# Causal mask added on VectorE with the maximum; loads in a new order; 37 warm-up matmuls instead of 27

## The chip, the cores and the metric

The kernel runs on one core of a Trainium2 chip. The metric is the device time of one execution in microseconds (us), the median of several runs. The engines of the core work in parallel, each through its own list of instructions in order: TensorE (PE) multiplies matrices, VectorE (DVE) and ScalarE (ACT) do element-wise work and reductions, GpSimd (POOL) small helpers, and SyncE (SP) issues most transfers from the main memory (HBM). PE writes its results to PSUM; everything else lies in SBUF.

## The reference

A decoder trunk of two layers for 256 positions of width 1024, in float32:

```python
for i in range(DEPTH):
    if i % N_MIXERS == 0:                    # layer 0: gated chunks
        u, v, q_mem = split(x @ a_w_in)
        mix = gmlp_mixer(u, v, ...)          # gelu(u) * (W_s LayerNorm(gelu(v)) + b) in chunks of 128
    else:                                    # layer 1: causal attention, 12 heads of 64
        q, k, v, q_mem = split(x @ b_w_in)
        mix = moba_attention(q, k, v)        # 256 positions are one key block: plain causal softmax
    mem_out = memory_cross_attention(q_mem, mem, w_mem_kv[i])   # 4 heads, 256 memory tokens
    sub = concat([mix, mem_out]) @ w_mix_out[i]
    x = layer_norm(ALPHA * x + sub, ...)
    x = layer_norm(ALPHA * x + swiglu(x, w_ffn_in[i], w_ffn_out[i]), ...)
```

In the causal attention a score counts only where the key's position is not behind the query's: `s_own = where(k_pos <= q_pos, s_own, -inf)`, then a softmax over the keys.

## The kernel before

Matrix products are made exact enough by splitting each float32 operand into a high and a low part: ACT rounds a raw tile to the high part (L370, `CAST`), DVE subtracts to get the low part (L371, `TENSOR_TENSOR`), and PE multiplies high by high, high by low and low by high. So each weight byte passes HBM, then ACT, then DVE, then PE. A class `Stream` loads weights in units of 1 MB (`raw_...`) into four raw buffers and splits them by halves into ten buffers (`spl_...`). A raw buffer is free again when DVE has done the low parts of both its halves.

The program, in the order of PE's work:

- 27 warm-up matmuls on a tile of zeros (L405).
- `va`: the v part of the first projection, 8 steps of 12 matmuls. Its weights and the transposed input come together in `raw_v0` to `raw_v3`, which fill the four raw buffers; `x0T` is the split input.
- `hqm` from unit `qm0` (queries of the memory attention; their split tiles are `qqm`), `pu` from `u0`, `u1`, `u2`, then `hkm` from `km0` (memory keys), `sv` (the spatial gating), the memory attention, and the output projection `opa` with units `o0_...`.
- the FFN of layer 0 (tiles ending in `f`), then layer 1: `bv`, `hqm` again, six rounds of two heads (`qk`, `s`, `pt`, `pv`), the output projection `opc`, and the FFN (tiles ending in `g`).

Besides the weights there are small inputs: the memory (`mraw` from `memT`, four loads of 256 KB), the spatial weights `wsT` (768 KB), scale and shift of the inner norm (`gv`), and six pieces of bias (`bs`). `memT` is needed by `hkm`, `wsT`, `gv` and the biases by `sv` and the steps around it.

In a round of the causal attention, `scores` computes for each of two heads a tile `s` in PSUM: the first 128 queries against keys 0 to 127 in columns 0 to 127, the other 128 queries against all 256 keys in columns 128 to 383. Columns 0 to 127 and 256 to 383 hold a triangle to be masked. The mask is `maskb`, 0 or -1e30 in bf16, added by one more matmul with the identity matrix `identb` that closes the accumulation. `Softmax` then takes the negated maximum of each part on DVE (`mb`), the exponential on ACT with that maximum as bias and with the sum of the row read out (`pb`, `zb`), and `normalise` scales by the reciprocal on DVE. The transposes `pt` of a round come a round later.

PE's order is the program's. The order of DVE, ACT and SP is set by three tables of numbers, `VECTOR_ORDER`, `SCALAR_ORDER` and `SYNC_ORDER`: each lists the instructions of its engine, by their number in the program, in the order in which they are to stand; `keep_order` enforces it. An instruction that waits therefore holds all that stand behind it.

Of the kernel before, what the change touches and what calls it, by code (L numbers as in the profile page):

```python
# [13 lines left out]
F32 = mybir.dt.float32  # L14
F32R = mybir.dt.float32r
BF16 = mybir.dt.bfloat16
AF = mybir.ActivationFunctionType
ALU = mybir.AluOpType
# [3 lines left out]
P = 128  # L22
# [10 lines left out]
WARM = 27  # L33
# [5 lines left out]
NEG = -1e30  # L39

# [147 lines left out]
class Stream:  # L188
# [169 lines left out]
def build(nc, tc, ins, out):  # L358
    ET = mybir.EngineType
    with (  # L360
# [12 lines left out]
        def acc_tile(name):  # L373
            return ps.tile([P, 512], F32, tag="acc", name=name)

        def mm_tile(name):
            return ps.tile([P, 512], F32, tag="mm", name=name)

        def work_tile(name):
            return actp.tile([P, 512], F32, tag="work", name=name, bufs=9)  # L380

        def sm(name, n=1):
            return small.tile([P, n], F32, tag=f"sm{n}", name=name, bufs=2 if n > 2 else 8)
# [4 lines left out]
        def flat(s):  # L388
            return s.rearrange("p a b -> p (a b)") if len(s.shape) == 3 else s
# [3 lines left out]
        def mm(o, lhsT, rhs, start, stop, on=False):  # L393
            nc.tensor.matmul(o, lhsT, rhs, start=start, stop=stop, skip_group_check=on)  # L394
# [8 lines left out]
        wt = mm_tile("warmup")  # L403
        for i in range(WARM):
            nc.tensor.matmul(wt[:, :P], warm, warm, start=True, stop=True)  # L405
        ident = const.tile([P, P], F32, name="ident")
        make_identity(nc, ident)
        identb = const.tile([P, P], BF16, name="identb")
        nc.gpsimd.tensor_copy(identb, ident)
        maskb = const.tile([P, 1, P], BF16, name="maskb")  # L410
        nc.gpsimd.memset(maskb, 0.0)
        nc.gpsimd.affine_select(
            out=maskb, in_=maskb, compare_op=ALU.is_ge, fill=NEG, base=0,
            pattern=[[0, 1], [-1, P]], channel_multiplier=1)
# [46 lines left out]
        class LayerNorm:  # L461
            def __init__(self, tt, xres, acc, nm):
                self.tt, self.r, self.acc, self.nm = tt, xres[tt], acc, nm
                self.stats = sm(f"st{nm}{tt}", 18)
                self.n = 0
# [45 lines left out]
        class Softmax:  # L511
            def __init__(self, s, parts, nm):
                self.p, self.parts = work_tile(f"p{nm}"), parts
                self.z = sm(f"z{nm}", 2)
                m = sm(f"m{nm}", 2)
                if len({hi - lo for lo, hi in parts}) == 1:
                    nc.vector.tensor_reduce(m, s.rearrange("p (n k) -> p n k", n=len(parts)), AX.X, ALU.max, negate=True)
                else:
                    for i, (lo, hi) in enumerate(parts):
                        nc.vector.tensor_reduce(m[:, i:i + 1], s[:, lo:hi], AX.X, ALU.max, negate=True)  # L520
                for i, (lo, hi) in enumerate(parts):
                    nc.scalar.activation(self.p[:, lo:hi], s[:, lo:hi], AF.Exp, bias=m[:, i:i + 1], accum_out=self.z[:, i:i + 1])
# [346 lines left out]
        for i in range(4):  # L869
# [11 lines left out]
            out=wsT, in_=wsT, compare_op=ALU.is_ge, fill=0.0, base=0,  # L881
            pattern=[[0, 12], [1, P]], channel_multiplier=-1)
# [20 lines left out]
        for j in range(4):  # L903
            t = actp.tile([P, 2, 512], F32R, tag="hm", name=f"memT{j}", bufs=4)
# [12 lines left out]
        for jj in range(3):  # L917
# [7 lines left out]
            bias = bsB[jj].rearrange("p (j o) t -> p j o t", o=1).to_broadcast([P, 2, 2, P])  # L925
# [78 lines left out]
        def scores(hp):  # L1004
            st, kl = qks[hp]
            ss = []
            for par in range(2):
                s = acc_tile(f"s{hp}{par}")
                q, k = st[:, 0, par, :], st[:, 1, par, :]
                mm(s[:, 0:128], q[:, 0:128], k[:, 0:128], True, False)  # L1010
                mm(s[:, 0:128], q[:, 0:128], kl[:, par, 0:128], False, False)
                mm(s[:, 128:384], q[:, 128:256], k, False, False)
                mm(s[:, 128:384], q[:, 128:256], kl[:, par], False, False)
                mm(s.rearrange("p (b t) -> p b t", t=256)[:, :, 0:128], identb, maskb.to_broadcast([P, 2, P]), False, True)
                ss.append(s)
            return [Softmax(s, [(0, 128), (128, 384)], f"b{hp}{j}") for j, s in enumerate(ss)]
# [149 lines left out]
```

## Time and profile before

| | us |
|---|---|
| median of 3 runs | 576.11 (575.17 to 577.29) |
| the profiled execution, its own time | 576.19 |
| its span from first to last instruction | 574.5 |
| PE busy | 554.3 |
| DVE busy | 502.7 |
| ACT busy | 379.0 |
| POOL busy | 48.7 |

The times in rows of the profile are microseconds from the start of the span. A row of the timeline has the start, the duration, the engine, the line of the code, the operation, output and inputs, and in brackets how long the engine had been idle before and what released it. Rows that follow each other with the same form are merged (x46), and the duration is then that of all. `PEld` is PE's loading of weights, which runs beside its matmuls; `SPq` is SP issuing transfers. A row of windows has, for each engine, busy us and the number of instructions, and then the granted clock of PE (1.00 is full), the share of the DMA engines' time and the rate in GB/s.

### The profile page before, as it was taken

The page shows a single profiled execution, that of the slowest core. Times are in us where ns is not written, and L with a number is a line of the kernel's source. Part 1 is how long each engine was busy: PE and PEld are TensorE (multiplying, and loading weights), DVE is VectorE, ACT ScalarE, POOL GpSimd, SP SyncE. Part 2 cuts the span into 40 slices and gives each one's busy share as a digit, 9 for nine tenths or more (in the row PEclk, how much of TensorE's full clock was granted, in tenths as well). Part 3 has the DMA queues.
Part 4 walks back from the last instruction along what each step waited for, and adds up shares of the span by engine and source line. Part 5 has one row for each costly group of instructions (what it writes and reads, how often), then busy time and mean ns, then how long its engine had stood idle before and what let it go on. Part 6 is the DMA issues. An engine that isn't in the chain of part 4 may idle for free. (4 is left out here: it accounts for less than half of the span.)

```text
span 574.5 us, 8129 instructions
## 1 busy us (share of the span) xinstructions
PE 554.3 (96%) x3037; PEld 479.1 (83%) x3037; DVE 502.7 (88%) x665; ACT 379.0 (66%) x576; POOL 48.7 (8%) x62
## 2 busy tenths in 40 slices
PE   8799999999999999999999999999998999999994
PEld 7799978978888888888899999778787888888884
DVE  5588759999999999997988888469999999898986
ACT  6585565876777768684456887564858677685830
POOL 1100002010202010100000000010112020101001
PEclk9979999999999999999999999999999999999999
DMA  8998833739796959587378243055397959595702
GB/s 302 352 400 321 314 132 96 203 102 269 208 293 189 303 203 271 217 269 254 130 260 326 74 148 114 35 127 178 97 272 201 333 166 301 189 266 218 216 1 74
DMA packets 23496, 120.99 MB, mean 211 GB/s; under 512 B 2592, under 2 KB 4896, under 8 KB 13344
## 3 DMA queue, kind: packets, MB, share of 16 engines
q1 hardware_dynamic: 17264, 99.03, 44.8%
q0 software_dynamic: 5760, 20.97, 20.6%
q10 hardware_dynamic: 432, 0.46, 0.3%
q8 instruction: 24, 0.39, 0.3%
q14 instruction: 16, 0.13, 0.1%
HBM read 119.41 MB, written 1.05 MB: 210 GB/s over the span
## 5 line engine op out<-in xcount | busy, mean ns | idle before, releaser
L370 ACT CAST spl_s_M<-raw_s_T 128x1024 fp32r<-128x1024 f32 x80 | 82.1, 1051 | 33.8 <-DVE raw_s_T L250 25.2
L371 DVE TENSOR_TENSOR spl_s_M<-raw_s_T,spl_s_M 128x1024 fp32r<-128x1024 f32 x80 | 95.4, 1218 | 1.9 <-ACT spl_s_M L370 1.8
L371 DVE TENSOR_TENSOR spl_s_M<-raw_s,spl_s_M 128x1024 fp32r<-128x1024 f32 x60 | 71.6, 1218 | 1.1 <-ACT spl_s_M L370 1.1
L370 ACT CAST spl_s_M<-raw_s 128x1024 fp32r<-128x1024 f32 x60 | 61.0, 1051 | 10.9 <-DMA raw_s<-in_w 9.6
L394 PE MATMUL fof<-spl_w,htf 128*128 128x512 f32 x264 | 63.0, 390 | 0.0
L394 PEld LDWEIGHTS fof<-spl_w,htf 128*128 128x128 f32 x264 | 49.3, 188 | 10.2
L371 DVE TENSOR_TENSOR spl_w<-raw_w,spl_w 128x1024 fp32r<-128x1024 f32 x44 | 53.3, 1218 | 1.2 <-ACT spl_w L370 1.1
L394 PE MATMUL fog<-spl_w,htg 128*128 128x512 f32 x228 | 54.2, 390 | 0.0
L394 PEld LDWEIGHTS fog<-spl_w,htg 128*128 128x128 f32 x228 | 42.7, 188 | 8.8
L250 DVE TENSOR_TENSOR raw_s_T<-raw_s_T,raw_s 128x1024 f32<-128x1024 f32 x40 | 48.5, 1218 | 0.1
L370 ACT CAST spl_w<-raw_w 128x1024 fp32r<-128x1024 f32 x44 | 45.5, 1050 | 1.2 <-PE fof L394 1.1
L394 PE MATMUL qk<-x2T,spl_qk 128*128 128x256 f32 x288 | 37.0, 285 | 0.0
L214 POOL DMA_DIRECT2D raw_s<-in_w x20 | 17.2, 858 | 233.9 <-DVE spl_s_M L371 231.7
L394 PEld LDWEIGHTS qk<-x2T,spl_qk 128*128 128x128 f32 x288 | 35.2, 191 | 0.6 <-DVE spl_o L371 0.4
L394 PE MATMUL Xg<-spl_s_M,x3T 128*128 128x512 f32 x120 | 29.0, 390 | 1.8 <-DVE htg L371 1.8
L394 PE MATMUL Zf<-spl_s_M,SfM 128*128 128x512 f32 x120 | 29.0, 390 | 1.3 <-DVE hf L713 1.3
L394 PE MATMUL Xg<-spl_s_M,SgM 128*128 128x512 f32 x120 | 29.7, 395 | 0.2 <-DVE SgM L371 0.2
L394 PE MATMUL Xf<-spl_s_M,SfM 128*128 128x512 f32 x120 | 29.4, 394 | 0.0
L394 PE MATMUL Xf<-spl_s_M,x1T 128*128 128x512 f32 x120 | 29.0, 390 | 0.0
L394 PE MATMUL Zg<-spl_s_M,SgM 128*128 128x512 f32 x120 | 28.9, 389 | 0.0
L394 PEld LDWEIGHTS Xg<-spl_s_M,x3T 128*128 128x128 f32 x120 | 22.4, 188 | 6.9 <-DVE htg L371 2.3
L394 PEld LDWEIGHTS Zf<-spl_s_M,SfM 128*128 128x128 f32 x120 | 22.4, 188 | 6.3 <-DVE hf L713 1.7
(261 smaller groups left out, 1102.5 us busy)
## 6 DMA issues: line engine op xcount, KB each, us to landing
raw_w<-in_w SPq DMA_DIRECT2D x22, 1024.0 KB, 8.1
raw_s<-in_w SPq DMA_DIRECT2D x20, 1024.0 KB, 8.2
raw_s_T<-in_w SPq DMA_DIRECT2D x10, 1024.0 KB, 7.7
raw_s_T<-in_w POOLq DMA_DIRECT2D x20, 512.0 KB, 8.7
raw_s<-in_w POOLq DMA_DIRECT2D x20, 512.0 KB, 5.8
raw_o<-in_w SPq DMA_DIRECT2D x8, 1024.0 KB, 6.2
raw_qk<-in_w SPq DMA_DIRECT2D x6, 1024.0 KB, 4.9
raw_v<-in_w SPq DMA_DIRECT2D x7, 512.0 KB, 8.2
```

What stands on the lines that cost most here:

```text
L214: self.nc.gpsimd.dma_start(self.raw[name][:, sl], self.unit_ap(other)[:, sl], accum_op=ALU.add)
L250: self.nc.vector.tensor_add(raw, raw, self.raw[used[1]][:, sl])
L370: nc.scalar.copy(hi, src)
L371: nc.vector.tensor_sub(lo, src, hi.bitcast(F32))
L394: nc.tensor.matmul(o, lhsT, rhs, start=start, stop=stop, skip_group_check=on)
```

## The change

Three things change.

The causal mask is no longer added by PE. `mask` is a float32 tile of three blocks of 128 columns, with the triangle in the first and the last and zeros in the middle, made on POOL. `Softmax` gets it for the causal attention: one DVE operation per part computes `(s + mask) * -1`, writes it to the tile `p` in SBUF and takes the minimum of it over the row into `m`. The exponential then reads `p` with scale -1 instead of reading `s`. The softmax of the memory attention stays as it was.

```diff
-        identb = const.tile([P, P], BF16, name="identb")
-        nc.gpsimd.tensor_copy(identb, ident)
-        maskb = const.tile([P, 1, P], BF16, name="maskb")
-        nc.gpsimd.memset(maskb, 0.0)
+        mask = const.tile([P, 3, P], F32, name="mask")
+        nc.gpsimd.memset(mask, 0.0)
         nc.gpsimd.affine_select(
-            out=maskb, in_=maskb, compare_op=ALU.is_ge, fill=NEG, base=0,
-            pattern=[[0, 1], [-1, P]], channel_multiplier=1)
+            out=mask[:, 0:3:2, :], in_=mask[:, 0:3:2, :], compare_op=ALU.is_ge, fill=NEG, base=0,
+            pattern=[[0, 2], [-1, P]], channel_multiplier=1)
...
-            def __init__(self, s, parts, nm):
+            def __init__(self, s, parts, nm, mask=None):
...
-                if len({hi - lo for lo, hi in parts}) == 1:
+                scale = 1.0
+                if mask is not None:
+                    scale = -1.0
+                    for i, (lo, hi) in enumerate(parts):
+                        nc.vector.tensor_tensor_reduce(self.p[:, lo:hi], s[:, lo:hi], mask[:, lo:hi], -1.0, BIG,
+                                                       ALU.add, ALU.min, m[:, i:i + 1])
+                    s = self.p
+                elif len({hi - lo for lo, hi in parts}) == 1:
...
-                    nc.scalar.activation(self.p[:, lo:hi], s[:, lo:hi], AF.Exp, bias=m[:, i:i + 1], accum_out=self.z[:, i:i + 1])
+                    nc.scalar.activation(self.p[:, lo:hi], s[:, lo:hi], AF.Exp, bias=m[:, i:i + 1], scale=scale,
+                                         accum_out=self.z[:, i:i + 1])
...
-                mm(s[:, 128:384], q[:, 128:256], kl[:, par], False, False)
-                mm(s.rearrange("p (b t) -> p b t", t=256)[:, :, 0:128], identb, maskb.to_broadcast([P, 2, P]), False, True)
+                mm(s[:, 128:384], q[:, 128:256], kl[:, par], False, True)
                 ss.append(s)
-            return [Softmax(s, [(0, 128), (128, 384)], f"b{hp}{j}") for j, s in enumerate(ss)]
+            return [Softmax(s, [(0, 128), (128, 384)], f"b{hp}{j}", flat(mask)) for j, s in enumerate(ss)]
```

There are ten more warm-up matmuls, and the three tables of orders are new; two lines of them as an example:

```diff
-WARM = 27
+WARM = 37
...
+BIG = 3e38
...
 SYNC_ORDER = (
-    0, 1, 2, 3, 4, 5, 6, 7, 8, 16, 17, 18, 19, 20, 14, 15, 21, 9, 22, 23, 24, 25, 26, 10, 11, 12, 13, 27, 28, 29, 30,
+    0, 1, 2, 3, 4, 5, 6, 7, 8, 9, 10, 11, 12, 16, 17, 13, 18, 19, 20, 14, 15, 27, 21, 22, 28, 23, 24, 25, 26, 29, 30,
```

On SP's queue, the loads behind the last `raw_v`. Before:

```order
L433 DMA raw_v3_242<-in_w 128x1024 x2
L871 DMA mraw0_298<-in_memT 128x2x256
L871 DMA mraw1_300<-in_memT 128x2x256
L871 DMA mraw2_302<-in_memT 128x2x256
L871 DMA mraw3_304<-in_memT 128x2x256
L879 DMA wsT_307<-in_wsT 128x1536
L866 DMA gv_295<-in_a_ln_v_g 128x768
L867 DMA gv_295<-in_a_ln_v_b 128x768
L887 DMA wsT_307<-in_bs 64x256
L232 DMA raw_qm0_279<-in_w 128x2048
```

After:

```order
L432 DMA raw_v3_250<-in_w 128x1024 x2
L233 DMA raw_qm0_287<-in_w 128x2048
L233 DMA raw_u0_289<-in_w 128x2048
L233 DMA raw_u1_291<-in_w 128x2048
L233 DMA raw_u2_293<-in_w 128x2048
L879 DMA mraw0_306<-in_memT 128x2x256
L879 DMA mraw1_308<-in_memT 128x2x256
L233 DMA raw_km0_301<-in_w 128x2048
L879 DMA mraw2_310<-in_memT 128x2x256
L879 DMA mraw3_312<-in_memT 128x2x256
L887 DMA wsT_315<-in_wsT 128x1536
L874 DMA gv_303<-in_a_ln_v_g 128x768
```

Four weight units now stand ahead of every small input, and `km0` ahead of half of `memT`; the biases come later still, between `vm0` and the first `o0` units.

On ACT, the same place: its list behind the last split of the input `x0T` (`vn` is the activation of `va`). Before:

```order
L370 CAST memT_571<-mraw_304 128x512
L894 ACT_TABLE_LOAD
L894 ACTIVATE vn<-va_75 128x384
L894 ACTIVATE vn<-va_77 128x384
L894 ACTIVATE vn<-va_76 128x384
L370 CAST spl_qm_0_287<-raw_qm_279 128x1024
L370 CAST spl_qm_1_290<-raw_qm_279 128x1024
L894 ACTIVATE vn<-va_78 128x384
L370 CAST spl_u_0_386<-raw_u_281 128x1024
```

After:

```order
L371 CAST spl_qm_0_295<-raw_qm_287 128x1024
L371 CAST spl_qm_1_298<-raw_qm_287 128x1024
L371 CAST spl_u_0_394<-raw_u_289 128x1024
L371 CAST spl_u_1_409<-raw_u_289 128x1024
L371 CAST spl_u_0_453<-raw_u_291 128x1024
L371 CAST spl_u_1_468<-raw_u_291 128x1024
L902 ACT_TABLE_LOAD
L902 ACTIVATE vn<-va_75 128x384
L902 ACTIVATE vn<-va_76 128x384
L371 CAST spl_u_0_512<-raw_u_293 128x1024
L371 CAST spl_u_1_527<-raw_u_293 128x1024
L371 CAST memT_570<-mraw_306 128x512
```

The splits of `qm0`, `u0` and `u1` moved ahead of the activation of `va`, those of `memT` behind it; DVE's list follows the same pattern.

On DVE, the last round of the causal attention (heads 10 and 11: tiles `s50`, `s51`), after:

```order
L605 TENSOR_TENSOR klm_132<-qk51_3508,qks5_3461 64x256
L520 ISA pb50_3608,mb50_3610<-s50_3598,mask_127 128x128
L520 ISA mb50_3610 128x1
L520 ISA pb50_3608,mb50_3610<-s50_3598,mask_127 128x256
L520 ISA mb50_3610 128x1
L520 ISA pb51_3615,mb51_3617<-s51_3603,mask_127 128x128
L520 ISA mb51_3617 128x1
L520 ISA pb51_3615,mb51_3617<-s51_3603,mask_127 128x256
L520 ISA mb51_3617 128x1
L533 RECIPROCAL zb50_3609<-zb50_3609 128x2
```

Where four `TENSOR_REDUCE` rows stood there are now eight: each new operation is followed by a row of one element per partition that reads the minimum out. The place of the round among its neighbours is the same.

58 rows, old and new, of tables (SCALAR_ORDER, SYNC_ORDER, VECTOR_ORDER) are left out of this document.

## Prediction

> **What bounds the kernel now.** I read the page first, then TensorE's own waits, then the timeline of the first 46 us, since the longest wait lies there.
>
> ```profile
> PE 554.3 (96%) x3037; PEld 479.1 (83%) x3037; DVE 502.7 (88%) x665; ACT 379.0 (66%) x576; POOL 48.7 (8%) x62
> ...
> PEclk9979999999999999999999999999999999999999
> DMA  8998833739796959587378243055397959595702
> ```
>
> TensorE (PE) works in 96% of the span; VectorE (DVE) has 88% and is second. The granted clock dips in the third slice (28.7 to 43.1 us) and nowhere else, and the DMA engines are nearly full only in the first slices. So I ask where PE stands still.
>
> ```profile
> PE hqm L394 <- ACT spl_qm L370: 3.0, 1, 3.0
> PE Xg L394 <- DVE htg L371: 1.8, 1, 1.8
> PE va L394 <- ACT x0T L370: 1.8, 1, 1.8
> PE Zf L394 <- DVE hf L713: 1.3, 1, 1.3
> PE hqm L394 <- DVE spl_qm L371: 0.8, 1, 0.8
> ```
>
> The columns are total us, times, longest. Two of the five rows are one place: `hqm`, the first memory-query projection, which waits for the two halves of its weights `qm0`, 3.0 + 0.8 us. PE around it:
>
> ```profile
> 1.05 3.06 PE L405 MATMUL warmup<-warm 128*128 128x128 bf16 x27 [1.05 <-DVE mhalf L402]
> 5.88 19.73 PE L394 MATMUL va<-spl_v,x0T 128*128 128x384 f32 x96 [1.77 <-ACT x0T L370]
> 28.58 0.50 PE L394 MATMUL hqm<-x0T,spl_qm 128*128 128x256 f32 x2 [2.96 <-ACT spl_qm L370]
> 29.84 8.45 PE L394 MATMUL hqm<-x0T,spl_qm 128*128 128x256 f32 x46 [0.76 <-DVE spl_qm L371]
> 38.13 1.13 PE L394 MATMUL pu<-x0T,spl_u 128*128 128x256 f32 x8
> ```
>
> From the end of `va` (5.88 + 19.73 = 25.61) to the first `pu` (38.13) the 48 `hqm` matmuls take 12.5 us. Why they start late, and why they are slow:
>
> ```profile
> 5.92 3.94 SPq L871 DMA_DIRECT2D mraw<-in_memT  x4
> 8.69 0.42 DVE L371 TENSOR_TENSOR x0T<-raw_v,x0T 128x256 fp32r<-128x256 f32 x1
> 11.36 0.59 SPq L879 DMA_DIRECT2D wsT<-in_wsT  x1
> 16.04 0.34 SPq L232 DMA_DIRECT2D raw_qm<-in_w  x1
> 27.48 1.99 ACT L370 CAST spl_qm<-raw_qm 128x1024 fp32r<-128x1024 f32 x2 [1.51 <-DMA raw_qm<-in_w]
> 28.56 2.36 DVE L371 TENSOR_TENSOR spl_qm<-raw_qm,spl_qm 128x1024 fp32r<-128x1024 f32 x2 [0.64 <-ACT spl_qm L370]
> ...
> raw_qm<-in_w SPq DMA_DIRECT2D x1, 1024.0 KB, 11.4
> ```
>
> The load of `raw_qm` is issued at 16.04 behind the small inputs (`memT`, `wsT` and others) and lands 11.4 us later; ScalarE (ACT) and DVE then split it into a high and a low part.
>
> ```profile
> core 0: us, PE busy (x) PEld busy (x) DVE busy (x) ACT busy (x) POOL busy (x), PEclk, DMA share, GB/s
> 5.50:12.00 6.50, 6.12 (x19) 6.12 (x20) 5.20 (x9) 4.79 (x10) 0.00 (x0) 1.00 1.01 383
> 12.00:25.70 13.70, 13.62 (x79) 13.29 (x77) 8.30 (x14) 8.59 (x16) 1.55 (x1) 1.00 1.03 356
> 25.70:29.20 3.50, 0.50 (x2) 0.30 (x2) 2.77 (x6) 1.99 (x3) 1.25 (x1) 0.99 1.01 365
> 29.20:36.00 6.80, 6.16 (x29) 6.16 (x30) 5.41 (x6) 4.65 (x6) 0.00 (x0) 0.50 1.06 418
> ```
>
> After the pause the clock column reads 0.50 for 6.8 us: 6.16 / 29 = 0.212 us for each matmul. The first 12 us are slow too, although that column says 1.00 there: 6.12 / 19 = 0.322 us for each `va` matmul against 13.62 / 79 = 0.172 afterwards, and the warm-ups need 3.06 / 27 = 0.113 us for 128 columns. Durations are the better witness of the clock here.
>
> **The front: small inputs behind the first weights.** Same bytes, same number of loads, another order on SP's queue; `raw_qm` now stands right behind `raw_v`. It reuses the buffer of `raw_v0`, which is free when DVE ends its last split of it, at 8.69 + 0.42 = 9.1 instead of the 16.04 of before. With the same 11.4 us to landing that is 20.5; splitting took from 27.48 to 28.56 + 2.36 = 30.92, 3.4 us, so `qm0` is whole at 23.9, before `va` ends at 25.61. The wait of 3.0 + 0.8 goes and with it the reason for the slow clock. Price: the same 48 matmuls undisturbed take 5.9 us in layer 1:
>
> ```profile
> L394 PE MATMUL hqm<-x2T,spl_qm 128*128 128x256 f32 x48 | 5.9, 283 | 0.0
> L394 PE MATMUL s<-maskb,identb 128*128 128x256 bf16 x12 | 3.4, 283 | 0.0
> L520 DVE TENSOR_REDUCE mb<-s 128x1 f32<-128x256 f32 x12 | 5.0, 416 | 0.0
> L520 DVE TENSOR_REDUCE mb<-s 128x1 f32<-128x128 f32 x12 | 3.5, 292 | 3.6 <-PE s L394 3.4
> L597 DVE TENSOR_TENSOR klm<-qk,qks 64x256 fp32r<-64x256 f32 x12 | 5.0, 419 | 3.1 <-ACT qks L596 3.0
> L522 ACT ACTIVATION_READ_ACCUMULATOR pb<-s,mb 128x1 f32 x24 | 4.7, 197 | 0.0
> ```
>
> So the front is worth 12.5 - 5.9 = 6.6 us. What is late next? The units behind `qm0` come at 1 MB in 2.9 us (356 GB/s) while PE spends 5.9 us on each, so `u0` to `u2` gain on it. Of what was pushed back, `memT` is needed with `km0`, four projections after `va` (25.6 + 4 x 5.9 = 49.2), and `wsT`, `gv` one later (55.1). Ahead of or with them lie some 6.5 MB from 20.5 on, 19 us, so about 40. The added waits: on SP each of `raw_u0` to `raw_u2` waits until DVE has emptied one more `raw_v` buffer, and all small inputs queue behind that, which the 40 already contains within a few us; on ACT and DVE the splits of `u2`, `memT` and `km0` now stand behind the activation and statistics of `va`, so behind its end at 25.6, and are wanted at 43.3 at the earliest (25.6 + 3 x 5.9). Cost 0.
>
> **Ten more warm-ups.** 10 x 0.113 = 1.13 us on PE, in the 1.77 us in which it waits for the first `x0T`. Cost 0; if that input came over 0.6 us sooner, the rest would show. I count no gain for the likeliest case, for the reason given under the rivals.
>
> **The mask.** PE loses 12 matmuls of 256 columns. What one holds up is not its 283 ns (that is latency) but the start of the next:
>
> ```profile
> 329.38 0.28 PE L394 MATMUL s<-klm,qks 128*128 128x256 f32 x1
> 329.50 0.28 PE L394 MATMUL s<-maskb,identb 128*128 128x256 bf16 x1
> 329.54 0.31 PE L394 MATMUL s<-qks 128*128 128x128 f32 x1
> ```
>
> 329.54 - 329.50 = 0.04 us; at most it is what an `hqm` matmul of the same width takes, 5.9 / 48 = 0.123. So 0.5 to 1.5 us in all; I take 0.8, nearer the row of the thing itself. On DVE 24 maximum reductions (416 and 292 ns) become 24 operations that read the scores in PSUM, add the mask, write the sum and reduce. The nearest row with two inputs, `klm`, takes 419 ns for 256 elements, as long as the reduction: +0 for the main part. Each is followed by a second row that reads the result out: between nothing and the 197 ns of ACT's read-out, so 0 to 4.7 us; I take the middle, 2.4. [...] The cover:
>
> ```profile
> 319.00:369.50 50.50, 49.96 (x406) 45.57 (x405) 38.83 (x98) 39.58 (x111) 0.00 (x0) 1.00 0.30 105
> ...
> 369.24 0.55 DVE L527 TENSOR_SCALAR pb<-pb,zb 128x128 f32<-128x128 f32 x2
> ...
> 370.73 0.82 PE L1023 MATMUL pt<-ident,pb 128*128 128x128 f32 x6
> ```
>
> Over the rounds of scores DVE idles 50.5 - 38.8 = 11.7 us, and results are transposed a round later. The thinnest cover is the last pair of heads: scaled by 369.24 + 0.55 = 369.8, wanted at 370.73, 0.9 us. Four read-outs at 0.1 and a later first exponential add about 0.5. Cost 0; should the cover go, a few tenths once. ACT's exponential now reads SBUF instead of PSUM and no longer holds the scores' bank: 0. On POOL a cast goes and a memset grows, long before anyone asks.
>
> **The rest of the tables.** In both FFN stages some sums and splits change places by a few rows. The two FFN waits above (1.8, 1.3) keep the DVE rows ahead of them: 0, bounds -1.5 to +1.5. That the front's gain survives needs DVE not to be late on its own account:
>
> ```profile
> 80.00:100.00 20.00, 20.00 (x109) 16.23 (x108) 14.26 (x21) 11.43 (x15) 2.89 (x3) 1.00 0.36 117
> ...
> 360.00:378.00 18.00, 18.00 (x108) 14.17 (x107) 5.99 (x21) 6.87 (x23) 0.00 (x0) 1.00 0.19 65
> ```
>
> Before each of its full stretches DVE has slack (5.7 of 20 us, 12.0 of 18), held back by PE's buffers; so both stretches start earlier with PE.
>
> **Sum.** The profiled execution took 576.19 us (span 574.5), 0.08 over the median of three, 576.11. 576.19 - 6.6 - 0.8 = 568.8.
>
> **Rivals.**
> 1. The warm-ups do reach the clock. If `va` ran at 0.172 us from its start it would take 96 x 0.172 = 16.5 instead of 19.73: 3.2 us more, 565.6. `qm0`, whole at 23.9 with its first half sooner, would be just in time for a `va` that ends at 22.4. For it: 37 x 0.113 = 4.2 us of work and a gap of 0.64 instead of 1.77. Against it: in before, a gap this size (0.76 at 29.1) was followed by half clock up to 36.0, and `va` itself ran 6 us without a break before it became fast. [...] Chance 0.28.
> 2. The gain is given back: the front is bound by bytes (DMA share 1.01 to 1.06 from 5.5 to 36 us), and `hkm` or `sv` waits where `hqm` did, or a FFN stretch waits anew. For it: the full queue. Against it: the 9 to 15 us of margin worked out above, and DVE's slack. If it took all but the mask and the first microsecond: 576.19 - 0.8 - 1.0 = 574.4. Chance 0.10.
> 3. Slower: the new DVE operation is dear. Above 11.7 / 24 = 0.49 us extra a pair DVE would bound the rounds of scores; to end 3 us above before it must first eat the 7.4 us: (11.7 + 7.4 + 3) / 24 = 0.92 us extra, some 1.3 us a pair. At 1.4 us extra: 568.8 + 24 x 1.4 - 11.7 = 590.7. For it: no row of before shows this operation. Against it: rows of its size take 0.29 to 0.42. Chance 0.03.
>
> The rest, 0.59, is my forecast, with 567 to 570.5 as its own range. A difference under 0.5% (2.9 us, 573.2 to 579.0) can hardly be told from none. Faster: 0.59 + 0.28 and a third of rival 2, 0.90; same 0.07; slower 0.03. The range runs from rival 1 with 1 us off to a partial rival 2: 564.5 to 572.0.
>
> **What would show it.** In the changed profile: no wait of `hqm` for `spl_qm`; a clock column without 0.50 around 29 to 36; `pu` starting near 31.5 instead of 38.13; SP's `raw_qm` near 9; no `maskb` rows; DVE busy 2 to 3 us more; attention without new PE waits. It is wrong if `hqm` still waits over a microsecond, if `sm`, `sv` or `hkm` shows a new wait, or if the pairs on DVE take over 0.8 us.

## The result, and the profile after

| | before | after |
|---|---|---|
| median, us | 576.51 (575.17 to 577.29, 4 runs) | 567.34 (567.07 to 568.78, 4 runs) |
| the profiled execution, us | 576.19 | 568.78 |
| its span, us | 574.5 | 567.1 |

The ratio is 0.9848, with a 95% interval of 0.9823 to 0.9874: some 8.8 us less, against 7.4 predicted. (Before has a fourth run here, 576.92, so its median is another than in the table ahead of the prediction.) The changed code has other line numbers (PE's L394 is now L395, DVE's splits L372, the mask operation L520). The page of after, engines and clock:

```profile
PE 550.7 (97%) x3035; PEld 474.7 (84%) x3035; DVE 502.6 (89%) x689; ACT 379.8 (67%) x576; POOL 48.7 (9%) x61
...
PEclk9999999999999999999999999999998999999999
```

The dip of the third slice is gone; a smaller one has come up in slice 31. DVE's busy time has not grown although it has 24 instructions more. PE's own waits (us in total, times, longest):

```profile
PE Xg L395 <- DVE htg L372: 1.8, 1, 1.8
PE Zf L395 <- DVE hf L721: 1.3, 1, 1.3
...
PE sm L395 <- DVE klm L605: 0.8, 2, 0.5
...
PE va L395 <- ACT x0T L371: 0.4, 1, 0.4
...
PE sm L395 <- ACT kkm L604: 0.2, 1, 0.2
```

Both waits of `hqm` have gone. The two of the feed-forward stages stand as they were, and `sm`, the scores of the memory attention, has new ones. The first 46 us, from the timelines of PE, SP, ACT and DVE:

```profile
1.05 3.88 PE L406 MATMUL warmup<-warm 128*128 128x128 bf16 x37 [1.05 <-DVE mhalf L403]
5.31 17.47 PE L395 MATMUL va<-spl_v,x0T 128*128 128x384 f32 x96 [0.38 <-ACT x0T L371]
22.62 5.91 PE L395 MATMUL hqm<-x0T,spl_qm 128*128 128x256 f32 x48
28.37 17.44 PE L395 MATMUL pu<-x0T,spl_u 128*128 128x256 f32 x144
...
8.58 0.33 SPq L233 DMA_DIRECT2D raw_qm<-in_w  x1
17.65 2.00 ACT L371 CAST spl_qm<-raw_qm 128x1024 fp32r<-128x1024 f32 x2 [1.35 <-DMA raw_qm<-in_w]
18.73 2.36 DVE L372 TENSOR_TENSOR spl_qm<-raw_qm,spl_qm 128x1024 fp32r<-128x1024 f32 x2 [1.41 <-ACT spl_qm L371]
```

The load of `raw_qm` is issued at 8.58 instead of 16.04, its split is whole at 21.1, and `hqm` follows `va` without a pause and takes 5.91 us. `pu` starts at 28.37 instead of 38.13: 9.8 us earlier. From the end of `va` (22.78) to `pu` it takes 5.6 us instead of 12.5, which is 6.9 of it; the other 2.8 are `va`, which starts 0.6 earlier and is fast from its start. The same stretches as before by windows:

```profile
5.50:12.00 6.50, 6.42 (x35) 5.84 (x35) 4.66 (x9) 4.27 (x8) 0.00 (x0) 1.00 1.02 376
29.20:36.00 6.80, 6.80 (x59) 6.80 (x58) 6.71 (x10) 5.68 (x11) 1.55 (x1) 1.00 1.04 402
```

6.42 / 35 = 0.183 us for a `va` matmul where it was 0.322, and full clock from 29.2 to 36. A part of this is lost again 30 us later, at `sm`. First DVE of after, then PE of after, then the same places of before:

```profile
46.53 8.03 DVE L372 TENSOR_TENSOR spl_o<-raw_o,spl_o 128x1024 fp32r<-128x1024 f32 x7
54.59 0.42 DVE L605 TENSOR_TENSOR klm<-hkm,kkm 64x256 fp32r<-64x256 f32 x1
...
59.02 0.39 PE L395 MATMUL sm<-klm,qqm 128*128 128x256 f32 x1 [0.54 <-DVE klm L605]
59.80 0.38 PE L395 MATMUL sm<-kkm,qqm 128*128 128x256 f32 x1 [0.16 <-ACT kkm L604]
60.41 0.39 PE L395 MATMUL sm<-klm,qqm 128*128 128x256 f32 x1 [0.23 <-DVE klm L605]
...
63.74 2.46 PE L395 MATMUL opa<-spl_o,mix 128*128 128x512 f32 x10
```

```profile
62.31 0.42 DVE L597 TENSOR_TENSOR klm<-hkm,kkm 64x256 fp32r<-64x256 f32 x1
...
67.00 0.28 PE L394 MATMUL sm<-kkm,qqm 128*128 128x256 f32 x1
71.81 2.46 PE L394 MATMUL opa<-spl_o,mix 128*128 128x512 f32 x10
```

`klm` is the low part of layer 0's memory keys, from the projection `hkm`. In after, PE ends `hkm` at 51.5 but DVE first works off seven splits of `o0` in one go and reaches `klm` at 54.59, 2.7 us ahead of the first `sm` (57.25); in before the lead was 4.7 us (62.31 to 67.00). Four `klm` and the casts `kkm` between them take turns, so PE runs into them: from the first `sm` to the first `opa` (the output projection) after needs 63.74 - 57.25 = 6.5 us, before 71.81 - 67.00 = 4.8. That is 1.7 us given back.

Where first matmuls start, us from the start of the span (the gains are worked out from hundredths):

| place | before | after | gained so far |
|---|---|---|---|
| `pu` | 38.1 | 28.4 | 9.8 |
| first `sm` | 67.0 | 57.2 | 9.8 |
| `opa` | 71.8 | 63.7 | 8.1 |
| `bv`, layer 1 | 284.4 | 276.5 | 7.9 |
| first causal score `s` | 319.8 | 312.0 | 7.9 |
| `opc`, behind the attention | 362.2 | 353.4 | 8.9 |
| `fog`, last feed-forward | 421.1 | 412.0 | 9.0 |
| `last` | 558.2 | 550.8 | 7.4 |

The attention stretch shrinks from 42.4 to 41.4 us. The last row is particular to this one execution, the slowest of its four: PE waits 1.84 us for `htg` as it did before, but here the clock falls to half behind it (434.6 to 438.0).

```profile
433.99 4.62 PE L395 MATMUL Xg<-spl_s_M,x3T 128*128 128x512 f32 x12 [1.84 <-DVE htg L372]
```

Twelve `Xg` matmuls take 4.62 us; where the clock stays up (experiment 7) the same twelve take 2.88. The mean clock was 0.995 in this execution and 0.997 to 0.998 in the other three, which ran 567.07 to 567.36.

The mask operation itself, from the groups of after (busy us, mean ns, idle before):

```profile
L520 DVE CUSTOM_DVE_ANT_0 pb<-s,mask 128x256 f32<-128x256 f32 x12 | 5.0, 420 | 0.0
L520 DVE CUSTOM_DVE_ANT_0 pb<-s,mask 128x128 f32<-128x128 f32 x12 | 3.5, 291 | 3.5 <-PE s L395 3.3
L520 DVE DVE_READ_ACCUMULATOR2_ANT mb<- 128x1 f32 x24 | 2.0, 83 | 0.0
```

### The profile page after: what moved, and what is told of

The parts are those of the page before. It is cut to its first block, busy times and chain, and to the rows that moved or that the text cites. A ratio compares the mean times of both kernels' runs of the same rounds, so it can differ in the third digit from the quotient of the medians.

```text
span 567.1 us, 8138 instructions
## 1 busy us (share of the span) xinstructions
PE 550.7 (97%) x3035; PEld 474.7 (84%) x3035; DVE 502.6 (89%) x689; ACT 379.8 (67%) x576; POOL 48.7 (9%) x61
## 5 line engine op out<-in xcount | busy, mean ns | idle before, releaser
L372 DVE TENSOR_TENSOR spl_s_M<-raw_s_T,spl_s_M 128x1024 fp32r<-128x1024 f32 x80 | 96.0, 1219 | 4.7 <-ACT spl_s_M L371 4.4
L372 DVE TENSOR_TENSOR spl_s_M<-raw_s,spl_s_M 128x1024 fp32r<-128x1024 f32 x60 | 71.7, 1219 | 1.7 <-ACT spl_s_M L371 1.7
L395 PE MATMUL fof<-spl_w,htf 128*128 128x512 f32 x264 | 63.0, 390 | 0.0
L395 PEld LDWEIGHTS fof<-spl_w,htf 128*128 128x128 f32 x264 | 49.3, 188 | 10.2
L395 PE MATMUL fog<-spl_w,htg 128*128 128x512 f32 x228 | 54.2, 390 | 0.0
L372 DVE TENSOR_TENSOR spl_w<-raw_w,spl_w 128x1024 fp32r<-128x1024 f32 x44 | 53.2, 1218 | 0.7 <-ACT spl_w L371 0.7
L395 PEld LDWEIGHTS fog<-spl_w,htg 128*128 128x128 f32 x228 | 42.7, 188 | 8.8
L395 PE MATMUL qk<-x2T,spl_qk 128*128 128x256 f32 x288 | 36.6, 284 | 0.0
L395 PEld LDWEIGHTS qk<-x2T,spl_qk 128*128 128x128 f32 x288 | 35.2, 191 | 0.6 <-issue 0.6
L395 PE MATMUL Xg<-spl_s_M,x3T 128*128 128x512 f32 x120 | 30.6, 406 | 1.8 <-DVE htg L372 1.8
L395 PE MATMUL Zf<-spl_s_M,SfM 128*128 128x512 f32 x120 | 29.0, 390 | 1.3 <-DVE hf L721 1.3
L395 PE MATMUL Xg<-spl_s_M,SgM 128*128 128x512 f32 x120 | 29.6, 394 | 0.2 <-DVE SgM L372 0.2
L395 PEld LDWEIGHTS Xg<-spl_s_M,x3T 128*128 128x128 f32 x120 | 23.6, 197 | 7.3 <-DVE htg L372 2.3
L395 PE MATMUL Xf<-spl_s_M,SfM 128*128 128x512 f32 x120 | 29.4, 394 | 0.0
L395 PE MATMUL Xf<-spl_s_M,x1T 128*128 128x512 f32 x120 | 28.9, 390 | 0.0
L395 PE MATMUL Zg<-spl_s_M,SgM 128*128 128x512 f32 x120 | 28.9, 389 | 0.0
L395 PEld LDWEIGHTS Zf<-spl_s_M,SfM 128*128 128x128 f32 x120 | 22.4, 188 | 6.4 <-DVE hf L721 1.7
```

What stands on the lines that cost most here:

```text
L372: nc.vector.tensor_sub(lo, src, hi.bitcast(F32))
```

## The experiments

Times of experiments go against runs of the kernel before on the same chip. Where a kernel's tables grew by lines, its line numbers are a few higher.

**1. The tables alone.** Before with after's three tables; mask by PE, 27 warm-ups.

```diff
 SYNC_ORDER = (
-    0, 1, 2, 3, 4, 5, 6, 7, 8, 16, 17, 18, 19, 20, 14, 15, 21, 9, 22, 23, 24, 25, 26, 10, 11, 12, 13, 27, 28, 29, 30,
+    0, 1, 2, 3, 4, 5, 6, 7, 8, 9, 10, 11, 12, 16, 17, 13, 18, 19, 20, 14, 15, 27, 21, 22, 28, 23, 24, 25, 26, 29, 30,
```

> The kernel before with the three new tables alone (mask by matmul, 27 warm-ups). Theory A (the front's order is worth 6.6 us by itself; the further 3.2 us seen in the changed kernel's va come from the warm-ups): 576.5 - 6.6 = 569.9, with va slow (about 19.7 us) and no wait of hqm. Rival B (the loads' order also made va fast, the warm-ups do nothing): 576.5 - 9.8 + 1.7 = 568.4 with a fast va (17.5 us).

569.6 us, ratio 0.9874 (0.9854 to 0.9894). `hqm` follows at once at 24.09, and `pu` starts at 29.84, 8.3 us earlier than before. 1.3 of that is `va`, which takes 18.39 us in this execution and 19.73 in before. `sm` waits here too, 0.6 us for `klm`, and from the first `sm` (58.72) to `opa` (65.09) it takes 6.4 us, so 1.6 are given back. The tables carry most of the gain, and the wait at `sm` comes with them.

**2. The mask alone.** After with before's tables and 27 warm-ups.

```diff
-WARM = 37
+WARM = 27
...
 SYNC_ORDER = (
-    0, 1, 2, 3, 4, 5, 6, 7, 8, 9, 10, 11, 12, 16, 17, 13, 18, 19, 20, 14, 15, 27, 21, 22, 28, 23, 24, 25, 26, 29, 30,
+    0, 1, 2, 3, 4, 5, 6, 7, 8, 16, 17, 18, 19, 20, 14, 15, 21, 9, 22, 23, 24, 25, 26, 10, 11, 12, 13, 27, 28, 29, 30,
```

> The kernel before with the mask added by DVE alone (old tables, 27 warm-ups). Theory A (attention is bound by PE, DVE's dearer step is covered): 12 matmuls less, 1.0 us less, 575.5. Rival B (the old order does not suit the longer DVE step, PE waits in the rounds): 576.5 to 579.

573.6 us, ratio 0.9951 (0.9934 to 0.9969): 2.4 us less by the medians, more than expected. The attention stretch is 41.3 us, 1.1 less than before's. The rest came at the front: the third slice of the clock row has an 8 in this execution and a 7 in before, and the 48 `hqm` matmuls are busy for 7.6 us instead of 9.0, so `pu` starts at 36.5 instead of 38.1. Whether the other three runs gained there too is not shown. That part cannot add to the tables', which remove that wait.

**3. The warm-ups alone.** Before with `WARM = 37`.

> The kernel before with 37 warm-ups alone. Theory A (va gets faster by up to 3.2 us, but hqm still waits for the load of qm0, which lands at the same time): va about 17.5 us, the wait of hqm about 3 us longer, 576.5 within 1 us. Rival B (the gain of va adds): 573.3.

575.6 us, ratio 0.9993 (0.9982 to 1.0004): nothing clear of noise. The warm-ups do reach the clock (from 5.5 to 12.0 a `va` matmul takes 5.82 / 30 = 0.194 us, in before 0.322), and the wait of `hqm` takes most of what they bring:

```profile
6.06 17.59 PE L394 MATMUL va<-spl_v,x0T 128*128 128x384 f32 x96 [1.18 <-ACT x0T L370]
27.69 0.50 PE L394 MATMUL hqm<-x0T,spl_qm 128*128 128x256 f32 x2 [4.05 <-ACT spl_qm L370]
```

`va` takes 17.59 us instead of 19.73, and the wait behind it 4.05 instead of 2.96. `raw_qm` is issued no sooner (16.62, before 16.04); it landed some 0.9 us sooner in this execution, its split starting at 26.59 instead of 27.48, and `pu` starts 0.9 earlier.

**4. After without the ten warm-ups.** After with `WARM = 27`.

> The changed kernel with 27 warm-ups. Theory A (the ten warm-ups bring the clock up before va): va slow again, 3.2 us longer, of which up to 1.7 us come back because the new wait of sm goes when PE is later there: 568.8 to 570.5. Rival B (the early clock was chance or came from the order): 567.3, no difference.

567.9 us, ratio 0.9853 (0.9831 to 0.9876): 0.5 us above after, which the intervals don't tell from nothing. `va` takes 19.15 us, `pu` starts 1.9 later than in after (30.23), `sm` too (59.1 against 57.2), but `opa` at 63.9 against 63.7. So in this execution what the warm-ups gain ends at `sm`: starting later, PE meets `klm` ready, whose first subtraction starts at 54.76, 4.3 us ahead of `sm`. The time lies under theory A's range, since `va` is 1.7 us longer and not 3.2, and nearly all of it comes back. It need not always come back: experiment 1, with the same lists and 27 warm-ups, has its first `klm` at 55.94, 2.8 us ahead of `sm`, and gives 1.6 us back. When `klm` is ready differs by over a microsecond between executions: in after the first subtraction starts at 54.59, in experiment 9, the same kernel, at 55.8.

**5. The order behind that.** After with `klm` and `kkm` of layer 0 ahead of the last splits of `o0` (41 to 44 are the four `klm` on DVE, 43 to 50 the eight `kkm` on ACT):

```diff
 VECTOR_ORDER = (
...
-    21, 45, 26, 39, 22, 40, 23, 37, 24, 38, 28, 46, 47, 49, 65, 50, 51, 48, 52, 66, 83, 84, 85, 86, 87, 88, 91, 41,
-    53, 92, 42, 54, 57, 43, 61, 55, 44, 56, 58, 67, 59, 60, 62, 68, 63, 69, 71, 64, 70, 72, 74, 73, 75, 77, 76, 78,
+    21, 45, 26, 39, 22, 40, 23, 37, 24, 38, 28, 46, 47, 49, 65, 50, 51, 48, 52, 66, 83, 84, 85, 86, 87, 41, 88, 42,
+    91, 43, 53, 92, 44, 54, 57, 61, 55, 56, 58, 67, 59, 60, 62, 68, 63, 69, 71, 64, 70, 72, 74, 73, 75, 77, 76, 78,
...
 SCALAR_ORDER = (
...
-    27, 20, 41, 21, 42, 39, 40, 22, 23, 30, 57, 58, 68, 69, 33, 70, 71, 72, 36, 77, 80, 43, 44, 81, 45, 46, 47, 48,
-    51, 52, 49, 50, 53, 54, 59, 60, 55, 56, 61, 62, 63, 64, 67, 65, 66, 86, 87, 73, 74, 75, 76, 78, 79, 96, 97, 107,
+    27, 20, 41, 21, 42, 39, 40, 22, 23, 30, 57, 58, 68, 69, 33, 70, 71, 72, 36, 77, 43, 44, 80, 45, 46, 81, 47, 48,
+    49, 50, 51, 52, 53, 54, 59, 60, 55, 56, 61, 62, 63, 64, 67, 65, 66, 86, 87, 73, 74, 75, 76, 78, 79, 96, 97, 107,
```

> The kernel after, with layer 0's four klm subtractions on DVE and their kkm casts on ACT moved ahead of the last spl_o splits. Theory A (the order of DVE's work gives back 1.7 us at sm): the sm<-klm and sm<-kkm waits (0.8 and 0.2 us) go, sm with pvm takes 4.8 us instead of 6.5, opa starts near 62.0 instead of 63.7, and the time is 567.3 - 1.7 = 565.6 us. Rival B (DVE simply has too much to do by then, so that the splits moved back become the next wait): opa waits for spl_o or mix, starts near 63.7 again, and the time stays 567.3 us.

566.1 us, ratio 0.9834 (0.9820 to 0.9847). No wait of `sm` for `klm` or `kkm` is left in the list of waits, and from the first `sm` (58.4) to `opa` it takes 4.8 us again:

```profile
53.54 0.42 DVE L607 TENSOR_TENSOR klm<-hkm,kkm 64x256 fp32r<-64x256 f32 x1 [1.08 <-ACT kkm L606]
...
63.22 3.14 PE L397 MATMUL opa<-spl_o,mix 128*128 128x512 f32 x13
```

The mechanism is as theory A has it, and rival B's next wait did not come. The start of `opa` moved by 0.5 us only, because in this execution `hqm` starts at 23.8 and not at 22.6, and `pu` 1.2 later than in after. By the time alone this can't be told from after, whose interval (0.9823 to 0.9874) overlaps. DVE's and ACT's lists were changed together, so how much each is worth is not shown.

**6. The same with 27 warm-ups.**

> The same as e5_klm with 27 warm-up matmuls instead of 37. Theory A (ten warm-ups start all that follows 1.9 us earlier, and only the klm wait hid it): 1.9 us above e5_klm, 567.5 us; sm near 59.1 and opa near 63.9. Rival B (something else between va and opa takes the gain of the warm-ups in any order): within 0.5 us of e5_klm.

567.6 us, ratio 0.9865 (0.9844 to 0.9886), 1.5 us above experiment 5 by the medians, though the intervals overlap slightly (0.9820 to 0.9847 and 0.9844 to 0.9886). `pu` starts 1.5 us later than in experiment 5 (31.1 against 29.5), and so does `opa` (64.8 against 63.2): with `klm` in time nothing takes the gain of the warm-ups between the two, as theory A has it.

**7. The wait of the last feed-forward.** After with `htg` of the second `tpg` two places earlier on each engine's list: on DVE (521) ahead of the second `spl_s_M` and one `spl_w`, on ACT (425) ahead of `u2g` and one `spl_w`; only these places change:

```diff
 VECTOR_ORDER = (
...
-    528, 530, 531, 532, 521, 533, 529,
+    528, 530, 521, 531, 532, 533, 529,
...
 SCALAR_ORDER = (
...
-    433, 434, 429, 436, 425,
+    433, 434, 425, 429, 436,
```

> The kernel after, with htg of layer 1's second tpg cast and subtracted before the second spl_s_M split instead of behind spl_w. Theory A (the one wait of the last feed-forward, Xg<-htg 1.8 us, is DVE's order alone): the wait goes, the half clock of 3.4 us that follows it in the profiled execution of after cannot follow, and the time is 567.3 - 1.8 = 565.5 us (566 if the splits moved back wait for 0.5). Rival B (the feed-forward is bound by loads and splits behind it): another wait of the same size at a later Xg or fog, 567.3 us.

566.7 us, ratio 0.9849 (0.9836 to 0.9862). In its list of waits `Xg<-htg` stands with 0.5 us in place of 1.8, and from the first `fog` to `last` it takes 135.8 us, against 137.1 to 137.3 where the wait stands without a clock dip (experiments 1, 4, 5, 9, 10 and 11). That is 1.4 us by the trace, and no wait of that size came up behind it; by the time alone it can't be told from after, whose runs it overlaps.

**8. Both orders.** The edits of experiments 5 and 7.

> The edits of e5_klm and e7_htg together. Theory A (two separate orders on DVE, the sum of both): 567.3 - 1.7 - 1.8 = 563.8 us, Xg<-htg and sm<-klm both without a wait. Rival B (an earlier start only makes the feed-forward wait longer for its loads): no better than the better one of the two, 565.5 us.

565.3 us, ratio 0.9819 (0.9802 to 0.9836). Neither `sm` nor `Xg` waits for over 0.6 us in one place. 1.5 us above theory A's figure, 0.2 under rival B's, so it was run again beside after (12).

**9. After once more,** with no edit.

> The kernel after once more, unchanged, as the base for the three beside it on the same chip. Theory A (the differences between e5 to e8 and after are the orders' own): 567.3 us within 0.7. Rival B (they come from the chip or the call): a time near e8_both's 565.3 us.

568.2 us (567.01 to 569.21), ratio 0.9860 (0.9835 to 0.9885): 0.9 above 567.3, so 0.2 outside theory A's bound, and on the far side from rival B's 565.3. Its profiled execution shows what the `klm` wait can cost beyond itself:

```profile
57.00:60.50 3.50, 2.25 (x15) 1.64 (x14) 3.41 (x6) 1.73 (x6) 0.00 (x0) 1.00 1.00 421
60.50:63.90 3.40, 3.37 (x14) 2.82 (x14) 3.31 (x8) 1.67 (x5) 0.00 (x0) 0.50 0.96 386
```

PE was busy for 2.25 of 3.5 us, the next 3.4 us ran at half clock, and `opa` started at 66.0 instead of 63.7.

**10. After without the mask edit.** Before with the new tables and 37 warm-ups.

> The kernel before with the new tables and 37 warm-ups, so after without the mask edit: PE still adds the mask by twelve matmuls. Theory A (what the mask edit is worth is the attention stretch alone, 42.4 us before and 41.4 after from the first s to the first opc): 1.0 us above e9_after, 568.3 us, with 42.4 us in that stretch and sm to opa as in after. Rival B (the edit also starts the front earlier, since e2_mask gained 2.4 us and its first input came 0.3 us earlier): 2 us or more above e9_after, 569.5 us.

569.7 us, ratio 0.9889 (0.9867 to 0.9911), 1.5 us above experiment 9 by the medians. That lies between theory A's 1.0 and rival B's 2, and the runs overlap (568.33 to 570.1 against 567.01 to 569.21), so the time does not decide; the profiles do. The stretch from the first `s` to `opc`, in this kernel:

```profile
312.90:355.30 42.40, 41.87 (x357) 38.95 (x355) 33.80 (x84) 35.16 (x95) 0.00 (x0) 1.00 0.35 125
```

and in experiment 9:

```profile
314.00:355.40 41.40, 40.78 (x346) 38.27 (x344) 33.84 (x104) 36.33 (x95) 0.00 (x0) 1.00 0.36 128
```

42.4 against 41.4, so 1.0 us, as theory A has it. It is the same in every profiled execution: 42.4 where PE adds the mask (before, experiments 1, 3 and 10), 41.3 to 41.4 in after and all others but experiment 11. Nor does the mask edit start the front earlier: `va` starts at 5.3 here as in after.

**11. The mask operation twice.** After, each of the 24 repeated; the tables got a second entry behind each, with the numbers above it raised.

```diff
                     for i, (lo, hi) in enumerate(parts):
-                        nc.vector.tensor_tensor_reduce(self.p[:, lo:hi], s[:, lo:hi], mask[:, lo:hi], -1.0, BIG,
-                                                       ALU.add, ALU.min, m[:, i:i + 1])
+                        for _ in range(2):
+                            nc.vector.tensor_tensor_reduce(self.p[:, lo:hi], s[:, lo:hi], mask[:, lo:hi], -1.0, BIG,
+                                                           ALU.add, ALU.min, m[:, i:i + 1])
```

> The kernel after with each of DVE's 24 mask operations issued twice, the second one a repeat: 24 more rows of 0.42 and 0.29 us, about 24 x 0.275 = 6.6 us of DVE's time by the distance to the next instruction (0.34 and 0.21 us). Theory A (DVE's step is covered: it idles 41.4 - 33.8 = 7.6 us in the attention stretch, and PE is the bound there): the stretch stays under 42.4 us and the time within 1 us of e9_after, 567.3 to 568.3 us. Rival B (the step lies on the chain s, mb, exponential, transposes that sets when PE goes on): the stretch grows by most of 6.6 us, 573 us.

568.5 us, ratio 0.9872 (0.9853 to 0.9890), 0.3 above experiment 9. The attention stretch of this kernel:

```profile
312.00:354.70 42.70, 41.46 (x346) 38.32 (x344) 39.74 (x139) 35.93 (x93) 0.00 (x0) 1.00 0.35 124
```

DVE works 39.74 of 42.70 us, 5.9 more than in after, and the stretch is 1.3 us longer, 0.3 over theory A's bound and far from rival B's. In after DVE's step is covered; doubled, it leaves 3.0 us of DVE's idle time in the stretch, and then it shows.

**12. Both orders beside after.**

> e8_both once more, beside after on the same chip. Theory A (the two orders are worth 1.7 and 1.3 us by the profiles): 2 to 3 us below e9_after, 564.8 us. Rival B (the gap between the medians of e8_both and after was one of chips): within 0.7 us of e9_after.

564.9 us (564.61 to 565.1), ratio 0.9810 (0.9792 to 0.9828), against 0.9860 (0.9835 to 0.9885) for after beside it: 3.2 us less by the medians, a little over theory A's 2 to 3, and the intervals don't meet. Theory A: the two orders together beat both kernels. In this profile `Xg<-htg` stands with 0.9 us, so a part of that wait remains.

## Why the prediction was right, point by point

The forecast of 568.8 us was 1.5 above the median, and faster was right. Its sum came out near for a reason that is partly luck: it left out two terms of opposite sign, 2.8 us gained by `va` and 1.7 lost at `sm`.

- **The front, 6.6 us: right, 6.9 measured.** `hqm` waits for nothing, runs at full clock in 5.91 us, and `raw_qm` is issued at 8.58 (forecast 9.1) and has landed by 17.65, so within 9.1 us and not 11.4; `qm0` is whole at 21.1 (forecast 23.9). Experiment 1, the tables alone, is worth 7.3 us by its ratio (6.1 to 8.4), but that holds 1.3 us of a faster `va` and 1.6 given back at `sm`. The step "What is late next?" looked at `qm0`, `memT` and `wsT` and was right on those: `hkm` and `sv` don't wait.
- **Ten warm-ups, 0: wrong at their place, and nearly right at the end.** The likeliest case took the gap before `va` to be enough to keep the clock low; it was rival 1 that happened, `va` 2.3 us shorter and 0.6 earlier, with `pu` 9.8 us sooner. Its 565.6 us was not reached, because `sm` took 1.7 back. The reason given against it, half clock after a gap of 0.76 us, failed: in before the clock record falls at 29.12, behind the wait of 2.96 us and with all but 0.04 us of the gap (29.08 to 29.84) still to come. The chance of 0.28 was the author's estimate, and no run shows its size; the runs showed this in its place: the 37 warm-ups take 3.88 us in after (4.2 in rival 1), and from the first start of `va` to its last it takes 17.0 to 18.1 us in eight profiled executions with 37 of them (after, experiments 3 and 7 to 12), 18.0 to 19.4 in four with 27 (before, experiments 1, 2 and 6).
- **No new wait at `sm`: wrong, 1.7 us.** The prediction named `sm` as a place that would show it wrong, but did not price it. Its step on the added waits ("on ACT and DVE the splits of `u2`, `memT` and `km0` now stand behind the activation and statistics of `va`") followed the order up to `km0` and stopped there; the seven splits of `o0` ahead of `klm` stood in DVE's new order. Experiment 5 takes that wait away by order alone. By the medians of experiments 4 and 6 the warm-ups pay 0.5 us with it and 1.5 without, but the first is within noise. It is rival 2 in small: a part of the gain was given back, at another place than `hkm` or `sv` and by the order of DVE's and ACT's lists.
- **The mask, 0.8: right in kind, a little small.** 1.0 us in the attention stretch between experiments 9 and 10 and 1.1 in experiment 2, by the profiles. By 1.0 / 12 = 0.083 us a matmul, the price lies between the 0.04 and 0.123 that were the bounds.
- **DVE's read-outs, 0 with 2.4 us more work: right at the end, the amount wrong.** The rows are 83 ns each, 2.0 us, but DVE's busy time stays at 502.6: a read-out lies in the tail of its operation, and the next mask operation starts with it:

```profile
322.05 0.29 DVE L520 CUSTOM_DVE_ANT_0 pb<-s,mask 128x128 f32<-128x128 f32 x1
322.26 0.08 DVE L520 DVE_READ_ACCUMULATOR2_ANT mb<- 128x1 f32 x1
322.26 0.42 DVE L520 CUSTOM_DVE_ANT_0 pb<-s,mask 128x256 f32<-128x256 f32 x1
```

  In these rows the pair is two instructions, and the second, 0.08 us, takes no time of its own: it and the next operation both start at 322.26.
- **The rest of the tables, 0 with bounds of 1.5: held.** From `opa` to `s` after loses 0.2 us and from `opc` to `fog` it gains 0.1. The FFN waits are the same rows.
- **One reading was wrong, and the sum does not rest on it.** The DMA engines are nearly full not only in the first slices: the row shows a 9 in eight later ones as well.

So the ledger of the profiled executions reads 6.9 + 2.8 - 1.7 + 1.0 = 9.0, as at `fog`, where the prediction had 6.6 + 0.8; the medians differ by 9.2.

## What to carry to other kernels

Work that starts earlier arrives at the next engine's old list: after pricing the wait that goes, walk on to the next places where PE takes something from DVE or ACT, and look in the new order at what that engine does just before. A part of a change that looks worthless (the warm-ups, ahead of a late load in experiment 3 and of a late `klm` in experiment 4) can pay once the wait that swallowed it is gone, so undo parts from the whole as well as adding them to the old. A short wait had a second price here, the clock: behind the wait of `Xg` for `htg`, 1.77 to 1.89 us, the twelve `Xg` matmuls took 4.62 and 4.61 us in after and experiment 6, and 3.02 to 3.06 in experiments 1, 4, 5, 9, 10 and 11.

## What the runs showed of the hardware

In before the clock record is at half from 29.12 to 35.95 (6.83 us), in after from 434.61 to 438.02 (3.41 us). The records of before start at 12.05, so a clock column of 1.00 ahead of that is only a missing record: a `va` matmul takes 0.322 us from 5.5 to 12.0 and 0.172 from 12.0 to 25.7. What makes the clock fall is not settled. Behind a wait of 1.84 us in after and one of 1.89 in experiment 6 twelve `Xg` matmuls took 4.62 and 4.61 us, with a mean clock of 0.79 from 432 to 440 in both; behind waits of 1.77 to 1.89 in experiments 1, 4, 5, 9, 10 and 11 they took 3.02 to 3.06. Three short waits of 1.25 us together (0.49, 0.15 and 0.61) in experiment 9 were followed by a clock of 0.50 from 60.5 to 63.9. What decides between these can't be read from the rows.
